# Weight sums of a ConvFFN by accumulating DMA in DRAM instead of on GpSimd, in a hybrid attention, retention and ConvFFN layer

## The chip, the core and the metric

The kernel runs on one core of one Trainium2 chip. The metric is device time in microseconds (us), the median of several runs. Engines are called as in the profile: PE (TensorE), PEld (its weight loads), DVE (VectorE), ACT (ScalarE), POOL (GpSimd) and SP (SyncE, which here only issues DMAs).

## The reference

One layer on 1024 latent tokens and 256 context tokens, D = 1024, all in float32: a modulated RMSNorm, one input projection that feeds a neighbourhood attention (8 heads of 64) and a retention in both directions (4 heads, 128 wide for q and k, 256 for v, chunks of 128), two projections merged by sigmoid gates, an output projection and a residual. Then the ConvFFN, which the change is about:

```python
def _conv_ffn(h, w_up, conv_w, conv_b, w_down):
    ...
    return (jax.nn.silu(a) * val) @ w_down
```

`a` and `val` are the two halves of `h @ w_up` (D_FF = 2816 columns each) after a depthwise convolution of width 3 along the tokens; a gated residual and a final RMSNorm follow.

## The kernel before, in words

**Precision.** Each float32 operand is split into a high and a low part (`split`: a cast on ACT, L86, and a subtraction on DVE, L87), and each product is three matmuls (high x high, high x low, low x high). A split needs the whole block in SBUF first: a load by SP, then L86, then L87, then PE.

**Strassen's scheme.** The gates, the up and the down projection multiply 2x2 blocks by seven products instead of eight. That needs sums of weight blocks and sums of activations. For the up projection `Seven.load` (L1379) loads four 128x512 blocks of w_up per unit through SP (`ur_load`) and POOL makes the four sums s1 to s4 (L1383 to L1386, tile `s`). The blocks and the sums of the up stage share a pool of 12 buffers (tag `r`). The first two of 22 units are computed plainly (`PLAIN`), 20 by Strassen; each has seven products (`step(0)` to `step(6)`) of 12 matmuls, PE line L1374, and the units are interleaved by `interleaved`: a unit's first product stands between the later products of the one before. `step(0)` copies product 0 out of PSUM on ACT (L1408, tile `pu`). `comb` makes the sums T1 to T4 of the activations ready for it, by loads from d_t into the same 12 buffers and splits (tile `T`). `conv` (L1754) makes the convolution, and for the down projection POOL makes four sums `sa` (L1777) for each second unit of the later half.

**Sums for the down projection.** They are made ahead and kept in DRAM (d_w): `down_sums` loads the four blocks of one of 11 units into tile `pj` through SP, POOL makes four differences (L1249), SP stores them. It is a generator, one sum a call. Five units are drawn in the retention, four in the gates, two in the ret projection.

**The retention** runs in slots (`slot`, L1262): 40 of them with a head's front part (`head.front`: projections to q, k, v, the rotary embedding `r`, states), beside which goes the mix part of the head before (`mix_a`, `mix_b`, `mix_c`: Q and O products, the normalisation `mvr`, `o`). Heads have 10 steps each (2 of context, 8 of latent tokens). At the end of a slot, one call of `next(ret_sums)` makes one down sum; it is left out in the context slots of heads 1 to 3 and in each head's last three. In a slot POOL has, in its order, the sum of `r` (L1115), the down sum, two sums `SS` (L1166) and `mvr` (L1193). DVE waits for `mvr` in L1194, and DVE's work for the next `r` (L1112 to L1114) stands behind that in its queue; ACT's `kz` (L1134) waits for `r`. Where heads change, the next head's weights (`in_w_ret`, 8 blocks a head, three buffers `raw`) are loaded through SP and split into `wc` and `wx` just in time.

Every DMA of the kernel before is issued by SP. Each engine executes its own instructions in order.

Of the kernel before, what the change touches and what calls it, by code (L numbers as in the profile page):

```python
# [16 lines left out]
P = 128  # L17
# [23 lines left out]
def tile_hybrid_layer(ctx, tc: tile.TileContext, io, dbg=None):  # L41
# [13 lines left out]
    d_ada = dram.tile([32, P], F32, name="d_ada")  # L55
    d_gate = dram.tile([2 * KB, 2, P, 512], F32, name="d_gate")
# [10 lines left out]
    cpool.tile([P, 24], F32, name="pad")  # L67
# [1168 lines left out]
    NH = NF // 2  # L1236

    def down_sums(pool_, j0, j1, bufs=8):
        def load(j, n):
            t = pool_.tile([P, 512], F32, tag="pj", bufs=bufs, name="pj")  # L1240
            sync.dma_start(t, io["w_down"][n % 2, NH * (n // 2) + j])
            return t

        ts, store = [load(j0, n) for n in range(4)], None
        yield
        for j in range(j0, j1):
            nxt = []
            for n, (c, x, y, o) in enumerate(((1, 1, 0, 0), (3, 3, 1, 1), (2, 3, 0, 3), (4, 2, 3, 2))):
                late(pool.tensor_tensor(ts[o], ts[x], ts[y], ALU.subtract))  # L1249
                if store:  # L1250
                    sync.dma_start(*store)
                store = (d_w[j, c - 1], ts[o])
                if j + 1 < j1:
                    nxt.append(load(j + 1, n))
                yield
            ts = nxt
        sync.dma_start(*store)

    RET_SUMS, GATE_SUMS = 5, 9
    ret_sums = down_sums(rt, 0, RET_SUMS)  # L1260

    def slot(main, mix, head=None, i=None):  # L1262
# [79 lines left out]
    def hx_sums(k):  # L1342
# [6 lines left out]
        for c, o, x, y in (("T1", b11, b12, b11), ("T3", b12, b22, b12), ("T2", b22, b22, b11), ("T4", b21, b21, b22)):  # L1349
            late(vec.tensor_tensor(o, x, y, ALU.subtract))  # L1350
# [25 lines left out]
    class Seven:  # L1376
        loaded = False

        def load(self):  # L1379
# [4 lines left out]
            pool.tensor_tensor(self.s2, self.s1, self.a11, ALU.subtract)  # L1384
            pool.tensor_tensor(self.s3, self.a11, self.a21, ALU.subtract)
            pool.tensor_tensor(self.s4, self.a12, self.s2, ALU.subtract)  # L1386
# [10 lines left out]
        def add(self, b, half, bank, x):  # L1397
            vec.tensor_tensor(self.dst(b, half), bank, x, ALU.add)
            self.done(b, half)

        def step(self, n):
# [7 lines left out]
            elif n == 1:  # L1409
                self.prod(self.Y, self.s2, "T2", True, False)  # L1410
                vec.tensor_tensor(self.u2, self.Y, self.p1, ALU.add)
            elif n == 2:
                self.prod(self.Z, self.s1, "T1", True, False)
            elif n == 3:
                self.fetch(1, 1)
                self.prod(self.Y, self.s3, "T3", False, False)
                vec.tensor_tensor(self.u3, self.Y, self.p1, ALU.add)  # L1417
                self.add(1, 1, self.Z, self.u3)
# [4 lines left out]
            elif n == 5:  # L1423
                self.fetch(1, 0)
                self.prod(self.Y, self.a22, "T4", False, True)
                self.add(1, 0, self.Y, self.p1)
            else:
                self.fetch(0, 1)
                self.prod(self.Z, self.s4, "B22", False, True)
                self.add(0, 1, self.Z, self.u2)  # L1430
# [104 lines left out]
    gate_sums = down_sums(gr, RET_SUMS, GATE_SUMS)  # L1535
    steps = interleaved(0, len(gu))
    n0, fetched = steps.index((len(gu) - 1, 0)), None
    for n, (i, k) in enumerate(steps):
        gu[i].step(k)
        if n % 3 == 1:  # L1540
            next(gate_sums, None)
# [12 lines left out]
    for _ in gate_sums:  # L1554
        pass
# [28 lines left out]
    pjp = sb("out_sums", "right")  # L1584
    out_sums = down_sums(pjp, GATE_SUMS, NH, 7)
# [25 lines left out]
    for db in range(2, KB):  # L1611
        wp[db] = pret_load(db)
        merge_load(db)
        if db == 2:
            brow(0, gate1)
        for half in range(2):
            pret(db, half)
            next(out_sums, None)
    pjp.release()
# [40 lines left out]
    def norm_out(tb, xr):  # L1660
# [25 lines left out]
        vec.tensor_tensor(b11, b12, b11, ALU.subtract)  # L1686
        vec.tensor_tensor(b12, b22, b12, ALU.subtract)
        vec.tensor_tensor(b22, b22, b11, ALU.subtract)
# [65 lines left out]
    def conv(j, gate, value):  # L1754
# [19 lines left out]
        for c, x, y, o in ((S1, a21, a22, ALU.add), (S2, S1, a11, ALU.subtract), (S3, a11, a21, ALU.subtract), (S4, a12, S2, ALU.subtract)):  # L1774
# [312 lines left out]
```

## Time and profile before

| what | value |
|---|---|
| time before, median of 3 runs | 1766.24 us (1765.4 to 1766.25) |
| span of the profiled execution | 1759.2 us, 7.0 us under the median |
| mean granted clock of PE | 0.996 |
| gates, ret projection | 768 to 921 us, 921 to 1008 us |
| plain up units, Strassen up units | 1101 to 1148 us, 1148 to 1540 us |
| down projection, end | 1540 to 1759 us |
| read from and written to DRAM | 187.34 MB, 69.48 MB |

The span is from the first to the last instruction of one profiled execution. Busy times are of single engines and overlap. A matmul of 128x512 has about 0.39 us in the rows, but a new one starts every 0.23 us, since they are pipelined. "DMA to landing" is the time from the issue of a transfer until its data are there. A name like `ur<-in_w_up` is output tile and input.

### The profile page before, as it was taken

Reading aid. Unit: us, or ns where it says so; the run is one execution under the profiler, and the core shown is the slowest. Engines: PE = TensorE matmul, PEld = TensorE weight load, DVE = VectorE, ACT = ScalarE, POOL = GpSimd, SP = SyncE. Lnnn points to the kernel's source line nnn. Section 1 sums busy time; section 2 is a strip of 40 time slices with the busy share of each in tenths; the row PEclk is TensorE's granted clock in tenths of the full one; section 3 lists DMA queues with packets and bytes.
Section 4 is the critical chain, followed back from the end, with each engine's and each line's share of the span. In section 5 each row is a group of like instructions: output and inputs, shape, how many; then the busy total and the mean of one; then the engine's idle time right before and its main releaser. Section 6 shows DMA issues by size and latency. Waiting matters only on the chain.

```text
span 1759.2 us, 24801 instructions
## 1 busy us (share of the span) xinstructions
PE 1726.0 (98%) x8405; PEld 1429.3 (81%) x8405; DVE 1284.2 (73%) x2454; ACT 849.2 (48%) x1826; POOL 539.3 (31%) x455
## 2 busy tenths in 40 slices
PE   8999999999999999999999999989999999999997
PEld 4688988888888888778888888778888888788886
DVE  4778887756776766777665557868899889875755
ACT  5666666653443434443444324534444444554444
POOL 1000000003334343555413300165555655211444
PEclk9999999999999999999999999999999999999999
DMA  9143334342231212677557733733322332586754
GB/s 348 61 130 125 95 117 147 117 133 87 73 108 43 72 42 68 203 238 239 200 199 268 246 143 132 254 108 102 108 90 92 118 120 90 170 296 192 239 162 162
DMA packets 139408, 261.10 MB, mean 148 GB/s; under 512 B 15856, under 2 KB 28304, under 8 KB 139280
## 3 DMA queue, kind: packets, MB, share of 16 engines
q1 hardware_dynamic: 139280, 259.51, 44.3%
q8 instruction: 66, 1.08, 0.3%
q14 instruction: 62, 0.51, 0.1%
HBM read 187.34 MB, written 69.48 MB: 146 GB/s over the span
## 4 chain that ended last, share of the span: by engine, by line
PE 43%; issue 6%; DVE 4%; POOL 3%; DMA 1%; ACT 1%; SPq 0%; POOLq 0%; ACTq 0%; DVEq 0%
PE u L1374 30%; PE y L1374 4%; PE pr L112 2%; PE pr L111 2%; PE pr L110 2%; PE om L122 1%; PE om L121 1%; PE om L123 1%; POOL x L1902 1%; DVE wc L87 0%; DVE b L1350 0%; DVE v L1679 0%; POOL pd L1939 0%; DVE hxT L87 0%; POOL x L1947 0%
## 5 line engine op out<-in xcount | busy, mean ns | idle before, releaser
L1374 PE MATMUL u<-T,wc 128*128 128x512 f32 x960 | 227.1, 392 | 5.1 <-ACT pu L1408 5.1
L1374 PEld LDWEIGHTS u<-T,wc 128*128 128x128 f32 x960 | 180.6, 189 | 45.7 <-ACT pu L1408 7.9
L1374 PE MATMUL y<-wc,ahl 128*128 128x512 f32 x924 | 210.6, 389 | 2.7 <-DVE wc L87 1.8
L1374 PEld LDWEIGHTS y<-wc,ahl 128*128 128x128 f32 x924 | 173.3, 188 | 39.7 <-DVE wc L87 2.5
L87 DVE TENSOR_TENSOR wc<-ur,wc 128x512 fp32r<-128x512 f32 x137 | 122.7, 897 | 65.8 <-ACT wc L86 65.8
L86 ACT CAST wc<-ur 128x512 fp32r<-128x512 f32 x137 | 85.0, 621 | 129.7 <-PE y L1374 72.3
L111 PE MATMUL mm<-low,wc 128*128 128x512 f32 (+1 forms) x328 | 124.0, 378 | 0.0
L1374 PE MATMUL u<-h2a,wc 128*128 128x512 f32 x480 | 112.3, 389 | 0.7 <-DVE pu L1417 0.7
L110 PE MATMUL mm<-hx,wc 128*128 128x512 f32 x264 | 107.4, 407 | 0.2 <-ACT wc L589 0.2
L1374 PEld LDWEIGHTS u<-h2a,wc 128*128 128x128 f32 x480 | 90.0, 188 | 19.8 <-DVE pu L1417 1.2
L112 PE MATMUL mm<-hx,wc 128*128 128x512 f32 x264 | 105.2, 399 | 0.0
L86 ACT CAST wc<-s 128x512 fp32r<-128x512 f32 x80 | 49.7, 623 | 93.2 <-PE u L1374 88.3
L123 PE MATMUL mm<-wc,low 128*128 128x512 f32 (+1 forms) x240 | 91.2, 380 | 0.0
L1374 PE MATMUL u<-hxT,wc 128*128 128x512 f32 x384 | 89.6, 389 | 0.0
L1508 POOL TENSOR_TENSOR col<-col,bcol 128x32 f32<-128x32 f32 x1 | 0.3, 253 | 280.7 <-DVE aw L538 280.7
L87 DVE TENSOR_TENSOR wc<-s,wc 128x512 fp32r<-128x512 f32 x80 | 83.5, 1046 | 3.8 <-ACT wc L86 3.4
L1374 PEld LDWEIGHTS u<-hxT,wc 128*128 128x128 f32 x384 | 72.1, 188 | 14.9
L87 DVE TENSOR_TENSOR wc<-raw,wc 128x512 fp32r<-128x512 f32 x92 | 68.0, 746 | 17.7 <-ACT wc L86 17.7
L121 PE MATMUL mm<-wc,hx 128*128 128x512 f32 x192 | 75.2, 392 | 0.6 <-ACT r L1105 0.6
L122 PE MATMUL mm<-wc,hx 128*128 128x512 f32 x192 | 75.2, 392 | 0.0
L1383 POOL TENSOR_TENSOR s<-ur 128x512 f32<-128x512 f32 x20 | 35.7, 1783 | 126.3 <-DVE wc L87 68.7
L86 ACT CAST wc<-raw 128x512 fp32r<-128x512 f32 x92 | 56.8, 621 | 33.0 <-PE pr L112 6.0
(393 smaller groups left out, 4671.3 us busy)
## 6 DMA issues: line engine op xcount, KB each, us to landing
ur<-in_w_up SPq DMA_DIRECT2D x80, 256.0 KB, 2.9
ur<-d_a SPq DMA_DIRECT2D x77, 256.0 KB, 3.1
aw<-in_w_ada SPq DMA_DIRECT2D x32, 512.0 KB, 3.3
pj<-in_w_down SPq DMA_DIRECT2D x44, 256.0 KB, 5.2
d_w<-pj SPq DMA_DIRECT2D x44, 256.0 KB, 2.0
d_a<-sa SPq DMA_DIRECT2D x44, 256.0 KB, 2.0
ur<-d_w SPq DMA_DIRECT2D x44, 256.0 KB, 3.8
d_a<-at SPq DMA_DIRECT2D x33, 256.0 KB, 2.7
```

The source lines that it names most:

```text
L86: act.copy(hi, src)
L87: (lo_eng or vec).tensor_tensor(lo, src, hi.bitcast(F32), ALU.subtract)
L110: pe.matmul(out, wh, xh, start=k == 0, stop=False)
L111: pe.matmul(out, wh, xl, start=False, stop=False)
L112: pe.matmul(out, wl, xh, start=False, stop=k == n - 1)
L121: pe.matmul(out, ah, bh, start=first, stop=False)
L122: pe.matmul(out, ah, bl, start=False, stop=False)
L123: pe.matmul(out, al, bh, start=False, stop=last)
L1374: pe.matmul(out, a, b, start=first and n == 0, stop=last and n == 2, skip_group_check=True)
L1383: pool.tensor_tensor(self.s1, self.a21, self.a22, ALU.add)
L1508: pool.tensor_tensor(col[:, 16:48], col[:, 16:48], bcol[:, 16:48], ALU.add)
L1902: pool.tensor_tensor(z, z, fg[:, gs(dh)], ALU.mult)
```

## The change

1. `down_sums` and its three uses are gone. `block_sums` takes their place: a job is four blocks and four places in DRAM; four plain DMAs copy blocks from DRAM to DRAM (`copy_of`, 16 rows of 16 KB, 256 KB each), and four accumulating DMAs add another block, or an earlier sum, onto them (`sum_of`, 32 rows of 8 KB). All eight are issued by POOL. The generator spreads each job over three rounds, so that an addition comes at least four issues after what it needs.
2. Twelve units of the up projection (`PRE`) and three of the down projection are such jobs in the retention, 15 x 8 = 120 issues, three in each of the 40 slots, context slots and last slots too. `puts` first copies 128x1 from the slot's `r0[i]` into a tile `tick` on POOL, which ties the issues to the slot, and then issues.
3. The other eight jobs of the down projection stand beside the up projection: after products 1 and 3 of each unit POOL copies 128x1 from `u2` or `u3` and issues two.
4. `Up.load` of those twelve units loads seven ready blocks (three of them raw, four from the new DRAM tensor `d_s`) through SP and gives POOL nothing to sum. The last eight units have POOL's four sums as before.
5. DMA can add but not subtract, so signs change: `block_sums` adds, and the sums of activations, the evacuations of products (`add`, u2, u3) and the end of the down projection add or subtract the other way. Their number and shapes stay.

```diff
+    d_s = dram.tile([12, 4, P, 512], F32, name="d_s")
...
-    cpool.tile([P, 24], F32, name="pad")
+    tick = cpool.tile([P, 24], F32, name="pad")[:, 0:1]
...
+    NH, PLAIN, PRE, RET_DOWN = NF // 2, 2, 12, 3
+    seq = [j + NH * i for j in range(NH) for i in range(2)]
+
+    def block_sums(jobs):
+
+        def add(out, src):
+            late(pool.dma_start(out, src, accum_op=ALU.add, max_dma_last_dim=8192))
+
+        def copy_of(n, c):
+            d, x, y, z, w = jobs[n]
+            late(pool.dma_start(d[c], (y, z, z, w)[c]))
+
+        def sum_of(n, c):
+            d, x, y, z, w = jobs[n]
+            add(d[c], (x, d[0], y, d[1])[c])
+
+        jobs = list(jobs)
+        for n in range(len(jobs) + 2):
+            for f, m, c in ((copy_of, n, 0), (sum_of, n - 1, 0), (copy_of, n, 2), (sum_of, n - 2, 3), (copy_of, n, 1), (sum_of, n - 1, 2), (copy_of, n, 3), (sum_of, n - 1, 1)):
+                if 0 <= m < len(jobs):
+                    yield f(m, c)
+
+    def up_jobs():
+        for n in range(PRE):
+            a = {(b, i): io["w_up"][seq[PLAIN + n], b, i] for b in range(2) for i in range(2)}
+            yield [d_s[n, c] for c in range(4)], a[1, 1], a[1, 0], a[0, 0], a[0, 1]
+
+    def down_jobs(j0, j1):
         for j in range(j0, j1):
...
+            b = {(r, c): io["w_down"][c, NH * r + j] for r in range(2) for c in range(2)}
+            yield [d_w[j, c] for c in range(4)], b[0, 0], b[0, 1], b[1, 1], b[1, 0]
+
+    def puts(it, src, n):
+        late(pool.tensor_copy(tick, src))
+        for _ in range(n):
+            next(it, None)
+
+    ret_sums = block_sums([*up_jobs(), *down_jobs(0, RET_DOWN)])
...
-            if i < NCB + NTB - 3 and (head.h == 0 or i >= NCB):
-                next(ret_sums, None)
+            puts(ret_sums, head.r0[i][:, 1, 0:1], 3)
...
+        def load(self):
+            n = self.n - PLAIN
+            if n >= PRE:
+                return super().load()
+            self.loaded = True
+            self.a11, self.s2, self.s1, self.s3, self.a12, self.a22, self.s4 = map(ur_load, (self.src[0, 0], d_s[n, 1], d_s[n, 0], d_s[n, 2], self.src[0, 1], self.src[1, 1], d_s[n, 3]))
...
+    up_sums = block_sums(down_jobs(RET_DOWN, NH))
     for i, n in interleaved(PLAIN, NF):
         units[i].step(n)
+        if n in (1, 3):
+            puts(up_sums, (units[i].u2 if n == 1 else units[i].u3)[:, 0:1], 2)
```

What stands in the engines' queues, at three places. First POOL in one retention slot with a mix part, before:

```order
L1115 TENSOR_TENSOR r_7262<-r_7262,r_7263 128x256
L1249 TENSOR_TENSOR pj<-pj 128x512
L1166 TENSOR_TENSOR SS<-st,SS 128x256
L1166 TENSOR_TENSOR SS<-run,SS 128x256
```

and such a slot after the change, from `r` to the next `r` (`pad` is the tile of `tick`; lines are those of the changed kernel, L1116 for L1115, L1167 for L1166, L1194 for L1193):

```order
L1116 TENSOR_TENSOR r_6264<-r_6264,r_6265 128x256
L1270 COPY pad<-r_6181 128x1
L1247 DMA d_s<-in_w_up 16x4096
L1243 DMA d_s<-in_w_up 32x2048
L1247 DMA d_s<-in_w_up 16x4096
L1167 TENSOR_TENSOR SS<-st,SS 128x256
L1167 TENSOR_TENSOR SS<-run,SS 128x256
L1194 TENSOR_TENSOR mvr<-mvr,mhalf 128x1
L1116 TENSOR_TENSOR r_6366<-r_6366,r_6367 128x256
```

The down sum between `r` and `SS` has given its place to the copy and three issues.

Second, SP at the start of the Strassen units, before, with what each row waits for (the last loads of the T sums, unit 2's four blocks, then unit 3's):

```order
L1735 DMA ur<-d_t 128x512 [waits DMAHW5_49,DVE_49]
L1735 DMA ur<-in_w_up 128x512 [waits DMAHW6_49,DVE_49]
L1735 DMA ur<-in_w_up 128x512 [waits DMAHW7_49,DVE_49]
L1735 DMA ur<-in_w_up 128x512 [waits DMAHW0_49,DVE_49]
L1735 DMA ur<-in_w_up 128x512 [waits DMAHW1_49,DVE_49]
L1766 DMA d_a<-at 128x512 [waits DMAHW2_49,DVE_49]
L1735 DMA ur<-in_w_up 128x512 [waits DMAHW6_49,DMAHW3_49,Pool_49]
```

and after (seven blocks of unit 2, then unit 3's first):

```order
L1739 DMA ur<-d_t 128x512 [waits DMAHW5_49,DVE_49]
L1739 DMA ur<-in_w_up 128x512 [waits DMAHW6_49,DVE_49]
L1739 DMA ur<-d_s 128x512 [waits DMAHW7_49,DMASW2_49,DVE_49]
L1739 DMA ur<-d_s 128x512 [waits DMAHW0_49,DMASW5_49,DVE_49]
L1739 DMA ur<-d_s 128x512 [waits DMAHW1_49,DMASW0_49,DVE_49]
L1739 DMA ur<-in_w_up 128x512 [waits DMAHW2_49,DVE_49]
L1770 DMA d_a<-at 128x512 [waits DMAHW3_49,DVE_49]
L1739 DMA ur<-in_w_up 128x512 [waits DMAHW4_49,Activation_49]
L1739 DMA ur<-d_s 128x512 [waits DMASW6_49,DMAHW5_49,DVE_49,Activation_49]
L1739 DMA ur<-in_w_up 128x512 [waits DMAHW6_49,DVE_49]
```

The wait for POOL (`Pool_49`) ahead of unit 3's first load is gone; waits for POOL's transfers of the retention (`DMASW`) stand at the loads from `d_s`.

Third, POOL beside the up projection after the change (before, four sums `s` a unit and the four `sa` stood here):

```order
L1270 COPY pad<-pu 128x1
L1243 DMA d_w<-d_w 32x2048
L1247 DMA d_w<-in_w_down 16x4096
L1270 COPY pad<-pu 128x1
L1243 DMA d_w<-in_w_down 32x2048
L1247 DMA d_w<-in_w_down 16x4096
...
L1781 TENSOR_TENSOR sa<-at 128x512
L1781 TENSOR_TENSOR sa<-sa,at 128x512
```

Each unit has two copies and four issues where its four sums were, until the last eight units, which keep them.

More of the change, by code (lines that the diff above doesn't have):

```diff
@@ L1233, in done @@
             return self.n >= NTB + 2
[L1236 to L1245, printed above, removed]
-        for j in range(j0, j1):
[L1247 to L1257, printed above, removed]
@@ L1938, in tile_hybrid_layer @@
         pool.tensor_tensor(u2[b], u2[b], gate2[:, gs(1)], ALU.mult)
-        pool.tensor_tensor(u2[b], u2[b], rows_of(b, 1), ALU.add)
+        pool.tensor_tensor(u2[b], rows_of(b, 1), u2[b], ALU.subtract)
     steps(4, range(NH), True, False)
```

47 lines of the change are left out of this document (17 added, 30 removed).

## Prediction, made blind

> **What bounds the kernel now.** I read the page's first part, then busy time by stage, then the waits of PE, and only then the other engines, in the stages that the change touches.
>
> ```profile
> span 1759.2 us, 24801 instructions
> PE 1726.0 (98%) x8405; PEld 1429.3 (81%) x8405; DVE 1284.2 (73%) x2454; ACT 849.2 (48%) x1826; POOL 539.3 (31%) x455
> ...
> 381.00:714.00 333.00, 331.69 (x1749) 283.53 (x1748) 226.38 (x716) 137.23 (x393) 115.04 (x150) 1.00 0.26 82
> ...
> 921.00:1008.00 87.00, 87.00 (x385) 72.07 (x384) 46.34 (x67) 35.21 (x60) 29.92 (x22) 1.00 0.76 256
> ...
> 1148.00:1540.00 392.00, 386.11 (x1689) 316.90 (x1688) 342.37 (x350) 178.87 (x250) 204.61 (x117) 1.00 0.35 113
> ```
>
> The last three rows are stages: the stretch, its length, the busy time of PE, PEld, DVE, ACT and POOL with counts, PE's granted clock, the DMA share and GB/s. PE is busy 98% of the span, so a sum that goes from POOL or SP is worth only the PE stall behind it. The retention (381 to 714 us) holds 1.3 us of PE idleness, the ret projection (921 to 1008), where down sums run now, none, the up projection (1148 to 1540) 5.9. Those 5.9 are one wait (row: who waited for whom, total, times, longest):
>
> ```profile
> PE u L1374 <- ACT pu L1408: 5.1, 1, 5.1
> ```
>
> The rows of that place are start, length, engine, line, operation, and in brackets the idle time ahead; first PE, then POOL, SP and ACT, and the clock in three stretches behind it.
>
> ```profile
> 1147.63 2.88 PE L1374 MATMUL u<-h2a,wc 128*128 128x512 f32 x12
> ...
> 1156.57 6.82 PE L1374 MATMUL u<-T,wc 128*128 128x512 f32 x22 [5.15 <-ACT pu L1408]
> ...
> 1139.52 5.42 POOL L1383 TENSOR_TENSOR s<-ur 128x512 f32<-128x512 f32 x1 [33.12 <-DMA ur<-in_w_up]
> 1145.02 1.72 POOL L1384 TENSOR_TENSOR s<-s,ur 128x512 f32<-128x512 f32 x1
> 1146.70 1.29 POOL L1385 TENSOR_TENSOR s<-ur 128x512 f32<-128x512 f32 x1
> ...
> 1148.02 8.22 SPq L1735 DMA_DIRECT2D ur<-in_w_up  x7
> ...
> 1146.78 1.87 ACT L86 CAST wc<-s 128x512 fp32r<-128x512 f32 x3 [4.78 <-POOL s L1384]
> 1152.85 0.62 ACT L86 CAST wc<-ur 128x512 fp32r<-128x512 f32 x1 [4.21 <-DMA ur<-in_w_up]
> ...
> 1155.93 0.58 ACT L1408 COPY pu<-u 128x512 f32<-128x512 f32 x1
> ...
> 1156.00:1158.00 2.00, 1.43 (x3) 1.16 (x4) 2.00 (x3) 1.03 (x3) 1.24 (x1) 0.62 0.47 122
> 1158.00:1160.00 2.00, 2.00 (x6) 1.59 (x5) 2.00 (x3) 0.00 (x0) 0.00 (x0) 0.53 0.51 137
> 1160.00:1165.00 5.00, 5.00 (x23) 4.13 (x22) 2.76 (x4) 1.25 (x2) 4.90 (x3) 1.00 0.39 145
> ```
>
> The first Strassen unit is late by its sums. POOL's first sum takes 5.42 us instead of 1.3 to 1.7. SP cannot send the next unit's loads until 1148.02, when POOL's third sum has let a buffer of the full pool go. ACT stands 4.78 us for the second sum, then 4.21 us for a load of the next unit, which stands in its queue ahead of the copy at 1155.93 that PE needs. PE idles 5.15 us and then runs at a granted clock of 0.62 and 0.53 until about 1160. Twelve matmuls at full clock take 2.88 us, a pitch of (2.88 - 0.39) / 11 = 0.226 us, so the 22 behind the stall should take 21 x 0.226 + 0.39 = 5.1 us and took 6.82. The wait thus costs 5.15 + 1.7 = **6.8 us**.
>
> The Trainium skill (TensorE: Matmul & The Clock Gate, Part 1: The HAM clock gate) says that a PE idle for a window of some 3.4 us falls to half clock. The 5.15 us gap followed by 0.53 agrees. By that rule a remainder of this stall under 3.4 us would cost its length alone.
>
> **The change, part by part.** *Up start.* Units 2 and 3 now load seven ready blocks each; no POOL sum and no release by POOL stands in SP's or ACT's way. Seven blocks of the first unit leave five of the twelve buffers to the second unit's loads, where four raw blocks, four sums and the wait for POOL stood. The order of PE's products is the same, and ACT's 4.78 and 4.21 us of idleness, 9.0 together, both go, which is more than the 5.15 that PE lost. What could be late next there are DVE's splits of the same tiles, which follow ACT's casts. I take the whole 6.8 us as the gain, with 0 as its other end.
>
> *Gates and ret projection.* PE has no idleness to give back there (87.00 of 87.00), so taking down sums, their loads and stores away is worth nothing.
>
> *Retention.* POOL gains three DMA issues and one 128x1 copy in each of 40 slots and loses a sum in 20. Here is one slot with a retention head beside another head's front; all its rows are POOL but the last two (DVE, PE). The fence behind it holds three groups: the sums of r over all four heads, the row nearest to the 128x1 copy (count, busy us, mean ns), and the only dynamic DMA queue.
>
> ```profile
> 496.64 0.73 POOL L1115 TENSOR_TENSOR r<-r,r 128x256 f32<-128x256 f32 x1 [2.11 <-DVE r L1114]
> 497.33 1.29 POOL L1249 TENSOR_TENSOR pj<-pj 128x512 f32<-128x512 f32 x1
> 500.36 0.73 POOL L1166 TENSOR_TENSOR SS<-init,SS 128x256 fp32r<-128x256 f32 x1 [1.75 <-ACT SS L1165]
> 501.05 0.74 POOL L1166 TENSOR_TENSOR SS<-run,SS 128x256 fp32r<-128x256 f32 x1
> 501.75 0.55 POOL L1193 TENSOR_TENSOR mvr<-mvr,mhalf 128x1 f32<-128x1 f32 x1
> 504.41 0.74 POOL L1115 TENSOR_TENSOR r<-r,r 128x256 f32<-128x256 f32 x1 [2.11 <-DVE r L1114]
> ...
> 502.33 0.41 DVE L1194 TENSOR_SCALAR o<-o,mvr 128x256 f32<-128x256 f32 x1 [0.98 <-POOL mvr L1193]
> ...
> 505.26 0.45 PE L121 MATMUL Q<-SS,qk 128*128 128x512 f32 x1
> ```
>
> ```profile
> L1115 POOL TENSOR_TENSOR r<-r,r 128x256 f32<-128x256 f32 x32 | 23.5, 735 | 115.1 <-DVE r L1114 115.1
> L1906 POOL TENSOR_SCALAR ssf<-ssf 128x1 f32<-128x1 f32 x8 | 3.0, 381 | 16.3 <-ACT xr L1897 16.3
> ...
> q1 hardware_dynamic: 139280, 259.51, 44.3%
> ```
>
> Between the end of r (497.37) and the start of SS (500.36) POOL has 2.99 us. The copy takes about 0.38 of it by the 128x1 row, which leaves 2.61 us for three issues, 0.87 us each. What one issue holds POOL for, call it X, no row shows: all 139280 packets went through the hardware queue. Past 0.87 us SS is late by 3X - 2.61; POOL's mvr comes straight behind SS, DVE's L1194 waits 0.98 us for mvr, and DVE's work for the next r is queued behind L1194, so the lateness adds up from slot to slot. PE first feels it when the sum of it passes the 505.26 - 501.79 = 3.47 us between SS and its use. Of 32 sums r, 24 are in slots of this kind (heads 1 to 3, eight in a row, with a long stretch between heads in which POOL catches up). The loss is 3 x (8 x (3X - 2.61) - 3.47): nothing up to X = 1.01, 13 us at 1.2.
>
> For X the lower end is SP's time for an issue, the upper the sum that POOL did in the slot, 1.29, or its mean over all 44, 1.43:
>
> ```profile
> 1140.20 0.33 SPq L1766 DMA_DIRECT2D d_a<-at  x1
> ...
> L1249 POOL TENSOR_TENSOR pj<-pj 128x512 f32<-128x512 f32 x44 | 62.7, 1426 | 7.5 <-DMA pj<-in_w_down 7.0
> ```
>
> An issue of 16 or 32 rows passes no 128x512 block through POOL; it is nearer to SP's 0.33 and to POOL's smallest instructions (0.38 and 0.55) than to 1.43. I take X at most 0.9 and the cost on this path as **0**, with 30 us (X = 1.43) as its far end.
>
> *Transfers in the retention.* 120 transfers of 256 KB, half of which also read their destination, add some (60 x 2 + 60 x 3) x 0.262 = 79 MB in 333 us, about 235 GB/s, to a stage that moved 82. The ret projection moved 256 without a PE stall, but at the change of heads PE waits directly for loads:
>
> ```profile
> PE mm L122 <- DVE wx L87: 0.7, 3, 0.2
> ...
> 518.04 1.25 ACT L86 CAST wc<-raw 128x512 fp32r<-128x512 f32 x2 [0.20 <-DMA raw<-in_w_ret]
> ...
> 523.62 0.63 ACT L86 CAST wx<-raw 128x512 fp32r<-128x512 f32 x1
> ...
> 524.68 0.68 DVE L87 TENSOR_TENSOR wx<-raw,wx 128x512 fp32r<-128x512 f32 x1
> ...
> 525.41 0.44 PE L122 MATMUL mm<-wx,hc 128*128 128x384 f32 x1 [0.22 <-DVE wx L87]
> ...
> DMA to landing us min/median/max: 2.5/2.6/3.7
> ```
>
> Two loads of in_w_ret follow each other through the same buffer, and PE waits 0.22 us at the end: there is next to no slack. Their landing times around this change are 2.5 to 3.7 us; the worst is 1.1 above the median. Before, the down sums were kept out of these slots; now they are not. Both loads at the worst give 2.2 us a change of heads, less the 0.43 us that lie between ACT's cast (until 524.25) and DVE's split (524.68), so 5.3 us over three changes; with none it is 0. POOL's transfers fill about half of a slot, so one load in two meets one: 1.1 - 0.43, three times, **2.0 us**.
>
> *Waits of the issues.* An accumulating transfer waits for the ones more than a slot (7.8 us) ahead of it. The nearest landings are
>
> ```profile
> pj<-in_w_down SPq DMA_DIRECT2D x44, 256.0 KB, 5.2
> d_w<-pj SPq DMA_DIRECT2D x44, 256.0 KB, 2.0
> ```
>
> 5.2 and 2.0 us, so POOL should not stand there. *Beside the up projection* POOL (204.6 of 392 us busy) loses 48 sums, at least 48 x 1.29 = 62 us, and gains 64 issues (58 at 0.9) and 40 copies (15): about even, with the sums of the last eight units needed long after their loads. I count nothing.
>
> **The sum.** 1759.2 - 6.8 + 2.0 = 1754.4 us of span. The median of the runs, 1766.2, is 7.0 us above the profiled span; I let that much lie around the new span too: **1761.4 us**.
>
> **Rivals.** *(a) POOL's issues stretch the retention slots*, the one that ends slower. It decides from X = 1.01; at 1.2 the kernel takes 1761.4 + 13 = 1774, at 1.43 1791. For it: POOL has already a sum of 5.42 us, against 1.3 to 1.7, when DVE was splitting T beside it, so POOL can be held up by DVE, and each slot has DVE at work. Against it: the sum in this slot took 1.29 us with DVE at work too. Spread evenly from 0.33 to 1.43, six tenths of X would lie under 1.01. *(b) The loads at the change of heads take the gain back*: 5.3 instead of 2.0 gives 1764.7. The 0.22 us waits speak for it; that the price takes the worst landing twice at each of three places speaks against. *(c) The stall at 1156 stays*, because another load or a DVE split comes as late: the change does not do there what it would; 1766.2 + 2.0 = 1768.2. Against it stand ACT's 9.0 us of idleness. *(d) DVE holds each issue for several times its length*: as the first sum was, 5.42 / 1.29 = 4.2 times, an issue of 0.55 us would take 2.3, and the loss be 3 x (8 x (6.9 - 2.61) - 3.47) = 93 us, 1854. The 1.29 us of the sum in this very slot speak against it. The Trainium skill (SBUF — State Buffer, SBUF: two separate sides) names such a hold: a GpSimd-issued DMA of about 620 ns takes about 3100 ns while a DVE copy keeps the shared port. No run shown so far has such an issue, so no number of mine rests on it.
>
> **How the numbers follow.** Forecast (1759.4 with no loss at the heads, to 1762.7) 0.48; (a) 0.22; (b) 0.20; (c) 0.06; (d) 0.04. A measurement of this kernel tells about 0.2%, 3.5 us, from no change, so the bounds are 1762.7 and 1769.8. Faster: the forecast, 0.48. Same: (b) and (c), 0.26. Slower: (a) and (d), 0.26. The range starts just under the case with no loss, 1759.4, and reaches into (a) to X = 1.33, 1784; what lies above is some 0.1, and some 0.1 below or in between is doubt in the terms themselves.
>
> **What would show it.** Right: no PE wait over 1 us at the start of the up projection and a clock of 1.00 there; POOL's gap from r to SS not longer than 2.99 us; the change of heads at most 1 us longer. Wrong: the slot's period over 7.8 us with PE waiting for SS or kz (a); PE waits of 1 to 2 us on wx or wc at each head (b); ACT again idle before the copy of pu (c).

## The result and the profile after

The changed kernel takes 1784.91 us (median; 1783.14 to 1794.34), the kernel before in the same comparison 1765.82. The medians differ by 19.1 us. The ratio of the runs is 1.0126, with an interval of 1.0100 to 1.0152, which is 18 to 27 us. The forecast of 1761.4 us was wrong in sign, and the time lies just above the range that ended at 1784.

These are the rows of the changed kernel that answer to those of before: the span and busy times, then the same three stages (retention, ret projection, Strassen units of the up projection; length, busy time of PE, PEld, DVE, ACT, POOL, PE's granted clock, DMA share, GB/s).

```profile
span 1784.1 us, 24998 instructions
PE 1734.6 (97%) x8405; PEld 1436.5 (81%) x8405; DVE 1245.1 (70%) x2454; ACT 850.3 (48%) x1826; POOL 537.7 (30%) x627
...
382.65:740.40 357.75, 340.22 (x1748) 290.41 (x1747) 215.46 (x716) 137.12 (x393) 175.90 (x290) 0.98 0.55 135
952.30:1039.30 87.00, 87.00 (x386) 72.03 (x385) 47.50 (x67) 35.68 (x60) 20.25 (x14) 1.00 0.65 210
1179.30:1564.70 385.40, 384.24 (x1687) 315.64 (x1687) 319.63 (x348) 176.89 (x247) 187.73 (x176) 1.00 0.58 177
```

The up projection went from 392.0 to 385.4 us, and PE idles 1.2 us there instead of 5.9. The retention went from 333.0 to 357.8: PE idles 17.5 us instead of 1.3, and its busy time grew by 8.5 because the clock fell to 0.98 on average. The ret projection is as long as before. Nearly the whole change of time lies in the retention, the up projection and one smaller place.

PE executes the same 8405 matmuls in all these kernels in nearly the same order, so the start of the n-th matmul in one trace less that in another shows where time went. Worked out so against the profiled execution of before, in us (bounds at 381, 714, 790, 921, 1140 and 1165 us of before; the experiments of the next section are already in it):

| kernel | to 381 | retention | to 790 | gates | to 1140 | start of up | rest |
|---|---|---|---|---|---|---|---|
| changed | +1.6 | **+24.9** | +1.0 | **+3.8** | -0.1 | **-6.9** | +0.2 |
| e1_tiny | -2.5 | +4.3 | -0.1 | +1.8 | -0.1 | -6.9 | +3.1 |
| e2_copies | -0.1 | +6.3 | -0.7 | +4.0 | 0.0 | -6.9 | +3.4 |
| e3_rows2k | +1.7 | +23.0 | +1.7 | +2.0 | +0.5 | -6.9 | +0.7 |
| e4_midhead | +2.0 | +15.6 | +1.5 | +1.7 | +0.3 | -6.9 | -0.5 |
| e5_mid3 | -1.2 | +1.2 | +0.7 | +4.1 | +0.1 | -6.9 | +3.8 |
| e6_nobunch | +0.3 | +25.0 | +2.6 | +4.2 | -0.1 | -6.9 | +0.9 |
| e7_lean2 | +0.9 | +1.7 | +0.6 | 0.0 | +0.3 | -6.9 | +1.5 |
| e8_lean4 | -0.9 | +19.2 | +0.6 | 0.0 | -0.2 | -6.9 | +1.2 |
| e9_pin | -0.7 | +23.5 | -0.9 | 0.0 | -0.1 | -6.9 | +0.8 |
| e10_nolast | +0.2 | +1.4 | +1.5 | +1.8 | -0.2 | -6.9 | +1.3 |
| e11_nolast_pin | +0.5 | +1.8 | +1.7 | 0.0 | +0.9 | -6.9 | +1.1 |

The first column is code that no kernel here changes; its -2.5 to +2.0 us shows what single executions differ by. The last column varies by 4 us among the kernels, and nothing is read from it.

**The start of the up projection** is as forecast. PE of the changed kernel there:

```profile
1178.90 2.88 PE L1387 MATMUL u<-h2a,wc 128*128 128x512 f32 x12
1181.62 8.39 PE L1387 MATMUL u<-T,wc 128*128 128x512 f32 x36
```

No bracket stands behind the second row: the 36 matmuls follow at once, (8.39 - 0.39) / 35 = 0.229 us apart. Before, the first 38 matmuls from the unit's start took from 1147.63 to 1163.39, 15.8 us; here 38 take 37 x 0.228 + 0.39 = 8.8.

**The retention.** First what PE waited for there (who, for whom, total, times, longest), then how POOL's slot looks now, as in the slot shown of before:

```profile
PE mm L122 <- ACT wc L87: 5.8, 3, 3.3
PE mm L122 <- ACT wx L87: 5.6, 2, 4.3
PE dS L122 <- ACT kz L1135: 4.5, 2, 2.4
PE Q L123 <- POOL SS L1167: 0.7, 1, 0.7
```

```profile
581.17 0.74 POOL L1116 TENSOR_TENSOR r<-r,r 128x256 f32<-128x256 f32 x1 [2.18 <-DVE r L1115]
581.85 0.19 POOL L1270 COPY pad<-r 128x1 f32<-128x1 f32 x1
581.97 0.58 POOL L1247 DMA_DIRECT2D d_s<-in_w_up  x1
582.55 0.83 POOL L1243 DMA_DIRECT2D d_s<-in_w_up  x1
583.08 0.81 POOL L1247 DMA_DIRECT2D d_s<-in_w_up  x1
584.64 0.74 POOL L1167 TENSOR_TENSOR SS<-init,SS 128x256 fp32r<-128x256 f32 x1 [0.75 <-ACT SS L1166]
```

The three issues start 0.58 and 0.53 us apart, and SS starts 3.47 us behind r (ready when ACT is), where it was 3.72. The issues fit. What doesn't is the change of heads; here the third one, first ACT, then PE, POOL's issues in it, and the landing of the loads around it:

```profile
607.73 1.27 ACT L87 CAST wc<-raw 128x512 fp32r<-128x512 f32 x2 [4.98 <-DMA raw<-in_w_ret]
...
617.45 0.62 ACT L87 CAST wx<-raw 128x512 fp32r<-128x512 f32 x1 [4.45 <-DMA raw<-in_w_ret]
...
608.40 0.69 PE L122 MATMUL mm<-wc,hc 128*128 128x384 f32 x1 [3.26 <-ACT wc L87]
618.12 0.62 PE L122 MATMUL mm<-wx,hc 128*128 128x384 f32 x1 [4.29 <-ACT wx L87]
...
605.10 0.81 POOL L1243 DMA_DIRECT2D d_s<-in_w_up  x1
...
608.68 1.07 POOL L1247 DMA_DIRECT2D d_s<-in_w_up  x1
...
DMA to landing us min/median/max: 2.6/7.2/8.3
```

Six transfers of POOL, of which the first and the last are shown, start within 4 us, the loads into `raw` land after 7.2 us in the middle and 8.3 at most (2.7 and 4.3 at this change before), ACT waits 4.98 and 4.45 us for them and PE 3.26 and 4.29. The waits for kz are the same thing once removed: at 449.68 ACT's cast, which stands ahead of kz in its queue, waits 2.18 us for such a load. Ahead of the other, at 691.47, a cast waits 3.69 us for a load of in_w_gate, the first weights of the gates.

```profile
449.68 0.62 ACT L87 CAST wc<-raw 128x512 fp32r<-128x512 f32 x1 [2.18 <-DMA raw<-in_w_ret]
```

By the starts of the matmuls the 24.9 us are 4.1, 4.7 and 10.1 at the three head changes and 6.0 at the end of the last head, where the gates' weights are loaded. They are of two kinds. PE's waits for wc, wx and kz, 15.9 us in the rows above, are the late loads. The other kind is PE's clock: five of these stalls, of 2.43, 2.09, 3.26, 4.29 and 2.02 us, are each followed by 3.4 us at half clock. PE loses half of such a spell, 1.7 us, if it is busy all through it, so five make some 8.5 us, the amount by which its busy time grew. Here are the spells behind the stalls of 2.43 and 2.02 us, and one behind a stall of 1.91 us in the gates (columns as in the stages above, the clock third from the end):

```profile
451.00:454.40 3.40, 3.40 (x13) 3.40 (x12) 1.53 (x4) 0.96 (x3) 1.38 (x3) 0.50 0.99 278
693.30:696.70 3.40, 3.40 (x11) 2.79 (x12) 2.06 (x5) 1.20 (x5) 1.16 (x2) 0.50 0.58 121
945.90:949.30 3.40, 3.40 (x9) 2.63 (x9) 1.40 (x3) 1.62 (x3) 0.00 (x0) 0.50 0.83 286
```

**The end of the gates** has a new stall, in a stage in which POOL issues no transfer: PE waits once for DVE's `pu`, and SP's queue ahead of that shows why. The last row is the same place in the queue of before.

```profile
PE u L1387 <- DVE pu L1430: 1.9, 1, 1.9
...
929.41 0.86 SPq L1540 DMA_DIRECT2D orw<-d_orr  x2
930.32 0.45 SPq L1487 DMA_DIRECT2D o<-d_pn  x1
936.47 0.32 SPq L1495 DMA_DIRECT2D d_gate<-c  x1
936.88 0.87 SPq L1540 DMA_DIRECT2D orw<-d_orr  x2
...
901.38 1.97 SPq L1527 DMA_DIRECT2D orw<-d_orr  x4
```

Two of four loads `orw` stand behind a store that waits until 936.47 for ACT; in the queue of before all four stood in a row. `pu` stands in DVE's queue behind the splits of these loads. The stall of 1.91 us and the 1.7 us of slow clock behind it make the 3.8 of the table. In the kernels with 1.7 to 2.0 in that column the stall was 1.42 to 1.74 us and no slow clock followed; in those with 4.0 to 4.2 it was 2.10 to 2.35 us and the clock fell.

### The profile page after: what moved, and what is told of

Its sections match the earlier page's. It is cut to its first block, busy times and chain, and to the rows that moved or that the text cites. A ratio compares the mean times of both kernels' runs of the same rounds, so it can differ in the third digit from the quotient of the medians.

```text
span 1784.1 us, 24998 instructions
## 1 busy us (share of the span) xinstructions
PE 1734.6 (97%) x8405; PEld 1436.5 (81%) x8405; DVE 1245.1 (70%) x2454; ACT 850.3 (48%) x1826; POOL 537.7 (30%) x627
## 3 DMA queue, kind: packets, MB, share of 16 engines
q0 software_dynamic: 7360, 48.25, 12.1%
## 4 chain that ended last, share of the span: by engine, by line
PE 38%; issue 6%; DVE 5%; POOL 3%; DMA 2%; ACT 2%; SPq 0%; POOLq 0%; ACTq 0%; DVEq 0%
PE u L1387 24%; PE y L1387 4%; PE pr L112 2%; PE pr L111 2%; PE pr L113 2%; PE om L123 1%; PE om L124 1%; PE om L122 1%; DVE wc L88 1%; POOL x L1913 1%; DMA raw<-d_orr 1%; PE u L112 1%; PE u L113 0%; PE u L111 0%; DVE ta L1765 0%
## 5 line engine op out<-in xcount | busy, mean ns | idle before, releaser
L88 DVE TENSOR_TENSOR wc<-ur,wc 128x512 fp32r<-128x512 f32 x185 | 149.5, 811 | 75.7 <-ACT wc L87 75.5
L87 ACT CAST wc<-ur 128x512 fp32r<-128x512 f32 x185 | 114.8, 622 | 178.3 <-PE u L1387 100.5
L1781 POOL TENSOR_TENSOR sa<-at 128x512 f32<-128x512 f32 x22 | 37.3, 1695 | 138.3 <-DVE at L1767 138.3
L112 PEld LDWEIGHTS mm<-low,wc 128*128 128x128 f32 x328 | 63.1, 192 | 6.9
L88 DVE TENSOR_TENSOR ahl<-ur,ahl 128x512 fp32r<-128x512 f32 x77 | 64.1, 840 | 0.8 <-ACT ahl L87 0.7
```

The costliest lines, as they stand in the source:

```text
L87: act.copy(hi, src)
L88: (lo_eng or vec).tensor_tensor(lo, src, hi.bitcast(F32), ALU.subtract)
L112: pe.matmul(out, wh, xl, start=False, stop=False)
L1781: pool.tensor_tensor(prev[c], x, y, o)
```

## The experiments

Theory T: the transfers make the loads of in_w_ret land late where heads change, and PE waits for those. Rivals: P, POOL's issues themselves hold up r and SS there; Q, the long rows of the transfers block the short rows of the loads. Each edit is against the changed kernel unless said otherwise. Single runs were compared with a run of the kernel before on the same chip.

### e1_tiny: the issues without their bytes

```diff
+            small = slice(0, 16) if tiny[0] else slice(0, P)
-            late(pool.dma_start(out, src, accum_op=ALU.add, max_dma_last_dim=8192))
+            late(pool.dma_start(out[small], src[small], accum_op=ALU.add, max_dma_last_dim=8192))
```

(the copies likewise with `tiny[1]`, both only in the retention; the kernel leaves out these sums, and its units read raw blocks in their place)

> The changed kernel with every one of the 120 transfers of the retention cut to its first 16 rows of 512 (32 KB instead of 256), so POOL issues as many DMAs at the same places but they move an eighth; the twelve units and the three down jobs then read raw weight blocks in place of the sums (the sums are left out). Theory T (the transfers make the loads of in_w_ret land late at the change of heads): landing times back to about 2.6 to 3 us, the three head changes back from 23 to 29 us to about 19.5, the kernel near 1763 (before less 6.8 for the start of the up projection, plus 3.6 for the new stall at the end of the gates). Rival P (POOL's issues, six in a row at a head change, hold up r and SS): head changes stay at 23 to 29 us and the kernel near 1784.

Measured: 1760.91 us (before: median 1763.25 of 7). The retention's loss falls from 24.9 to 4.3 us; loads of in_w_ret land after 2.9 us (group median, 4.6 in the changed kernel). POOL issues as often and at the same places. So P is out for some 20 of the 25 us. The rest is not pursued; here the largest wait of PE in the head changes is 1.1 us for DVE's split of wx.

```profile
raw<-in_w_ret SPq DMA_DIRECT2D x32, 256.0 KB, 2.9
...
PE mm L123 <- DVE wx L88: 2.3, 3, 1.1
```

### e2_copies: only the plain copies keep their bytes

The same edit with `tiny` for the accumulating transfers alone, so that seven eighths of each accumulation are left out.

> The changed kernel with only the 60 accumulating transfers of the retention cut to 16 rows of 512; the 60 plain copies stay at 256 KB (three of four sums are left out). Theory T with each transfer weighing by its bytes moved (copy 2, accumulation 3): about 40% of the loss in the retention stays, some 8 to 10 us of 24, kernel near 1772. If the accumulations alone make the loads late, the head changes go back to 19.5 us (kernel near 1763); if the copies do it, they stay (1782).

Measured: 1767.26 us; the retention loses 6.3 us, 2.0 more than with both kinds cut. The copies are the small part, smaller than the 8 to 10 us that weighing by bytes gave. The software queue of DMA shows the kinds apart (packets, MB, share of 16 engines' span), first the changed kernel, then this one, then e1_tiny:

```profile
q0 software_dynamic: 7360, 48.25, 12.1%
```

```profile
q0 software_dynamic: 6400, 34.48, 7.9%
```

```profile
q0 software_dynamic: 6400, 20.72, 5.4%
```

12.1% of 1784.1 us is 215.9 us of all engines, 7.9% of 1765.5 is 139.5, 5.4% of 1759.1 is 95.0. Cutting 60 accumulations to an eighth saves 76.4 us, so one holds all 16 engines for about 76.4 / (60 x 7/8) = 1.46 us, if an eighth of a transfer takes an eighth of the time; a copy 44.5 / 52.5 = 0.85. Since the loss grows from 6.3 to 24.9 when the accumulations come back, it isn't in proportion to the engines' time (44.5 us for 2.0 us of loss, 76.4 for 18.6); the queue that the loads meet may have to be long before PE feels it, which is argued, not shown. Accumulations without copies were not tried.

### e3_rows2k: short rows

```diff
-            late(pool.dma_start(out, src, accum_op=ALU.add, max_dma_last_dim=8192))
+            late(pool.dma_start(out, src, accum_op=ALU.add, max_dma_last_dim=2048))
```

(the copies likewise)

> The changed kernel with the same bytes, but each transfer of POOL in 128 rows of 2 KB instead of 16 of 16 KB or 32 of 8 KB. Theory Q (the large rows stand ahead of the 2 KB rows of the loads on each DMA engine): landing times of in_w_ret fall to 3 to 4 us and half or more of the 24 us of the retention returns, kernel 1765 to 1772. Theory T (bytes and time on the DMA engines count, not the row): no gain, 1783 or more, and more if 128 descriptors hold POOL longer than the 0.53 us of now (above 1.01 us the slots stretch as well).

Measured: 1783.98 us, the retention 23.0 us longer, in_w_ret landing after 4.4 us (4.6). The length of the rows doesn't matter here; Q is out. 128 rows didn't stretch the slots between the head changes either.

### e4_midhead: five issues a slot, away from the head changes

```diff
-            puts(ret_sums, head.r0[i][:, 1, 0:1], 3)
+            if i < NCB + NTB - 3 and (head.h == 0 or i >= NCB):
+                puts(ret_sums, head.r0[i][:, 1, 0:1], 5 if head.h else 6)
```

> The changed kernel with no POOL transfer in the slots around a change of heads (the slots that the down sums used before), five instead of three in each of the 15 others of heads 1 to 3 and six in the seven of head 0; one down job fewer there (14 jobs). Theory T: loads of in_w_ret land in about 2.6 us again at the change, head changes near 19.5 us, kernel near 1764; what five issues cost in the middle is 5 x 0.53 + 0.19 = 2.85 us against 2.99 of room, nothing. Rival: the middle slots now stretch or their loads come late, and the loss only moves: 1775 or more.

Measured: 1774.9 us (1772.89 to 1780.73), ratio 1.0075 [1.0048, 1.0102]. The second and third head change take 19.7 and 19.5 us again (from one r to the next), but the loss moved, as the rival said. POOL of this kernel in two slots of head 0 shows a wait that my prediction had put at nothing. Behind it stand PE's largest waits in the retention and, from the changed kernel, the group with most of its waits of this kind:

```profile
428.63 0.35 POOL L1270 COPY pad<-r 128x1 f32<-128x1 f32 x1
433.02 0.79 POOL L1243 DMA_DIRECT2D d_s<-d_s  x1 [4.05 <-DMA d_s<-d_s]
...
442.77 0.79 POOL L1243 DMA_DIRECT2D d_s<-d_s  x1 [3.70 <-DMA d_s<-d_s]
...
PE tp L1124 <- POOL r L1116: 5.5, 6, 1.8
PE tpo L1201 <- DVE A L1175: 2.8, 4, 1.1
...
L1243 POOL DMA_DIRECT2D d_w<-d_w x22 | 18.0, 819 | 12.1 <-DMA d_w<-d_w 12.1
```

With six issues a slot, as head 0 has them, an accumulation comes less than a slot after the one that it needs, POOL stands 4.05 and 3.70 us for that to land, and r behind it is late. In the changed kernel the spacing keeps this small, not at nothing: POOL stands five times for one of its own transfers, 12.7 us in all, four of these where a list of jobs ends and the spacing with it. Nearly all of that is hidden; PE waits 0.7 us behind it, once, for SS.

### e5_mid3: three issues a slot, away from the head changes

```diff
-    NH, PLAIN, PRE, RET_DOWN = NF // 2, 2, 12, 3
+    NH, PLAIN, PRE, RET_DOWN = NF // 2, 2, 6, 2
...
-            puts(ret_sums, head.r0[i][:, 1, 0:1], 3)
+            if i < NCB + NTB - 3 and (head.h == 0 or i >= NCB):
+                puts(ret_sums, head.r0[i][:, 1, 0:1], 3)
```

> The changed kernel with three POOL transfers a slot as it has, but none in the slots around a change of heads, and so only eight jobs in the retention (six units of the up projection instead of twelve, two down jobs instead of three; the rest of the sums as the change makes them, on POOL or beside the up projection). Theory T (late loads at the change of heads are the whole loss of the retention, and only transfers near them make them late): retention as long as before within 3 us, the start of the up projection 6.8 us shorter, the end of the gates 3.6 us longer, kernel 1 to 4 us under before on the same chip. Rival (any three transfers a slot cost, wherever they stand): retention 10 us or more longer, kernel slower than before.

Measured: 1763.68 us of 10 runs against 1764.06 of 15; ratio 0.9998 [0.9989, 1.0008]. The retention is as long as before (+1.2 us) with 64 transfers in it, so transfers away from the loads cost nothing there, within the 2 us by which executions differ. The 6.9 us at the start of the up projection are there; 4.1 at the end of the gates take most of them back, and the profiled execution has 3.8 more in the last column. The kernel is not faster than before; 1 to 4 us less were expected.

### e6_nobunch: none in the context slots

```diff
-            puts(ret_sums, head.r0[i][:, 1, 0:1], 3)
+            if head.h == 0 or i >= NCB:
+                puts(ret_sums, head.r0[i][:, 1, 0:1], 3)
```

(with PRE = 10, RET_DOWN = 2)

> The changed kernel with no POOL transfer in the two context slots of heads 1 to 3, which stand right behind a last slot of the head before; the last three slots of each head keep theirs (96 issues, ten units and two down jobs). Theory T by queueing (six transfers within 3 us at each change, 3 x 1.46 + 3 x 0.85 = 6.9 us of all DMA engines' time, stand ahead of the loads): the loads land at 5 us at most and half or more of the 26 us of the retention goes, kernel 1766 to 1773. Rival (any transfer near the loads does it, not the number in a row): more than two thirds stays, 1777 or more.

Measured: 1787.78 us, the retention 25.0 us longer. My own version of T fails: six in a row are not needed. The three head changes lose 20 of these 25 us, against 18.9 in the changed kernel. The other 5 come at the end of the last head, where POOL stands 4.60 us for its own accumulation to land and r is late, the cost that e4_midhead shows.

### e7_lean2: the kernel before with only two units summed by DMA

Against the kernel before: its `down_sums` stay on POOL where they were, and 16 issues for units 2 and 3 stand in head 0 (with the signs of the changed kernel).

```diff
+            if head.h == 0 and i < NCB + NTB - 3:
+                puts(ups, head.r0[i][:, 1, 0:1], 3)
             if i < NCB + NTB - 3 and (head.h == 0 or i >= NCB):
                 next(ret_sums, None)
```

> The kernel before, with its down sums on POOL where they were, and only the first two Strassen units of the up projection summed by POOL's DMAs, 16 issues in the first seven slots of head 0. If the start of the up projection needs only these two units and the gain does not hang on the rest of the change: 6 to 7 us less than before on the same chip, no new stall at the end of the gates (SP's queue there is as before) and the changes of heads at 19.5 us. If the third unit's sums on POOL come late instead, the stall moves there and the gain is under 3 us.

Measured: 1758.01 us (1755.55 to 1759.22) against 1764.06; ratio 0.9965 [0.9951, 0.9978], 6.2 us less. The gain of the change needs 16 of its 184 issues. The slots of head 0 have a down sum too, but no mix part beside it.

### e8_lean4: four units, in slots that also have a down sum

```diff
-            if head.h == 0 and i < NCB + NTB - 3:
-                puts(ups, head.r0[i][:, 1, 0:1], 3)
+            if i >= NCB and i < NCB + NTB - 3:
+                puts(ups, head.r0[i][:, 1, 0:1], 2)
```

(against e7_lean2, with PRE = 4; the slots of heads 1 to 3 have a mix part as well)

> As the run with two units, but four units summed by POOL's DMAs, 32 issues, two a slot in the five middle slots of each head. Theory T: these are away from the loads, so the same time as with two units, within 2 us. Rival: two issues and a POOL sum in one slot (2 x 0.53 + 0.19 + 1.29 = 2.5 us of 2.99) stretch the slots; 5 us or more slower than with two units.

Measured: 1774.33 us; the retention 19.2 us longer. The slots stretch, as the rival said, but not by the time of the issues. Here are POOL's slot, DVE's two operations for kz in it, PE's largest wait, and ACT's cast that SS waits for:

```profile
491.95 0.74 POOL L1116 TENSOR_TENSOR r<-r,r 128x256 f32<-128x256 f32 x1 [2.18 <-DVE r L1115]
...
493.36 0.72 POOL L1268 DMA_DIRECT2D d_s<-in_w_up  x1
493.88 1.51 POOL L1251 TENSOR_TENSOR pj<-pj 128x512 f32<-128x512 f32 x1
497.14 0.74 POOL L1167 TENSOR_TENSOR SS<-st,SS 128x256 fp32r<-128x256 f32 x1 [1.76 <-issue]
...
493.16 2.65 DVE L1136 SCALAR_TENSOR_TENSOR kz<-r,dec,kz 128x128 fp32r<-128x128 f32 x2 [0.96 <-ACT kz L1135]
...
496.62 0.40 ACT L1166 CAST SS<-st 128x256 fp32r<-128x256 f32 x1
...
PE tpo L1201 <- DVE A L1175: 10.6, 10, 2.1
```

POOL is free again at 495.39, in time for SS at 3.7 us behind r (495.65). But DVE's kz, which starts at 493.16 beside POOL's issues and its sum, takes until 495.81, just past the end of the sum. DVE's A stands behind it, PE waits for A, ACT's casts come late, and SS with them. The group of kz in the retention (72 times; busy, mean ns) tells it for three kernels, before, changed and this one:

```profile
L1135 DVE SCALAR_TENSOR_TENSOR kz<-r,dec,kz 128x128 fp32r<-128x128 f32 x72 | 36.4, 532 | 20.9 <-ACT kz L1134 20.7
```

```profile
L1136 DVE SCALAR_TENSOR_TENSOR kz<-r,dec,kz 128x128 fp32r<-128x128 f32 x72 | 26.3, 373 | 25.5 <-ACT kz L1135 25.1
```

```profile
L1136 DVE SCALAR_TENSOR_TENSOR kz<-r,dec,kz 128x128 fp32r<-128x128 f32 x72 | 60.0, 857 | 22.1 <-ACT kz L1135 21.9
```

With issues alone kz takes 373 ns in the mean, with sums 532, with both 857. These means mix cases. Single operations that overlap no work of POOL, or its issues alone, take about 0.35 us in all three kernels; one that overlaps a down sum takes 0.92 to 0.98 us in the kernel before; one that overlaps a down sum and an issue takes 1.8 to 3.8 us here, 15 times. So it is POOL's sum that holds DVE, not POOL's issue; why the two together hold it longest is open. The Trainium skill (SBUF — State Buffer, Who interferes with whom) says that DVE and GpSimd share one pair of ports, which only one of them holds at a time. The trace agrees as far as the sums go.

### e9_pin: the order at the end of the gates

```diff
-            fetched = orr_load(g_raw("orw"), 0, n - n0 - 1 + KH)
+            fetched = orr_load(g_raw("orw"), 0, n - n0 - 1 + KH, lambda ins: ins)
```

> The changed kernel with one edit: the four loads orw at the end of the gates keep the place in SP's queue where the program names them, instead of two of them behind a store that waits for ACT. If the 2 us stall at 945 us and the slow clock after it (3.6 us in all) come from that order, which moved when the gates' down sums left, they go: from the ret stage on about 3.6 us less than the changed kernel, the retention as late as in it. If they come from something else that the change moved, the step of 3.6 us at the end of the gates stays.

Measured: 1777.05 us (before: one run, 1766.08). The step at the end of the gates is 0.0 instead of 3.8, the retention still 23.5 longer. The order of SP's queue was the cause there.

### e10_nolast and e11_nolast_pin: none in the last three slots

```diff
-            puts(ret_sums, head.r0[i][:, 1, 0:1], 3)
+            if i < NCB + NTB - 3:
+                puts(ret_sums, head.r0[i][:, 1, 0:1], 3)
```

(with PRE = 8, RET_DOWN = 2; the second with the edit of e9_pin as well)

> The changed kernel with no POOL transfer in each head's last three slots, but with them in the context slots behind the change (84 of 120 places, 80 issues, eight units and two down jobs). The run that left out the context slots alone still lost 26 us, so the last three slots, where six of the eight loads of in_w_ret are sent, should hold most of the loss: landing times near 3 us for those loads and under a third (8 us) of the retention's loss left, kernel 1763 to 1770. If it needs both left out, as in the run where the retention was as short as before, the loss stays above 15 us and the kernel above 1775.

> Both repairs together: no POOL transfer in each head's last three slots (80 issues, eight units and two down jobs in the retention), and the four loads at the end of the gates in the order of the program. If the loads at the change of heads and that order are all that the change cost, what is left is the gain at the start of the up projection, 6.8 us, less about 1 us for a late r at the end of the last head: 5 to 7 us less than before on the same chip, as the kernel with two units. If transfers in the other slots or beside the up projection also cost something, the gain is under 3 us.

Measured: e10_nolast 1760.68 us (before: one run, 1766.08), less than the 1763 to 1770 expected, the retention 1.4 us longer than before; e11_nolast_pin 1759.96 us (1756.58 to 1762.69) against 1765.19, ratio 0.9967 [0.9955, 0.9980]. Landing of in_w_ret and PE's largest wait in the retention of e10_nolast:

```profile
raw<-in_w_ret SPq DMA_DIRECT2D x32, 256.0 KB, 2.8
...
PE tp L1124 <- POOL r L1116: 1.2, 1, 1.2
```

The 23.5 us of the retention come from 36 of 120 issues: those in the three slots of each head in which most of the next head's weights (in the last head the gates' first) are loaded. Transfers in the slots just behind do no harm. That total numbers don't explain it, e6_nobunch shows: its 96 issues, with those slots among them, lose all of it, and the 80 here next to nothing. Both repairs together leave 5.2 us between the medians, within the 5 to 7 expected, with eight units and two down jobs summed in the retention and the rest beside the up projection. e7_lean2 and e11_nolast_pin are both faster than both kernels and can't be told apart.

## Why the prediction was wrong, point by point

- **The start of the up projection**: -6.8 us forecast, -6.9 in all twelve kernels of the table. Right, with its second part: the 1.7 us of slow clock behind the 5.15 us stall went with it. PE waits 1.2 us in the whole up projection.
- **POOL's issues**: at most 0.9 us forecast, mostly 0.48 to 0.61 measured from the start of one issue to that of the next (0.53 in the middle), so X was below 1.01. Single slots shifted by up to 0.3 us, but in heads 1 and 2 the eight r take 55.0 us from first to last, as before. Right. What the term left out is that POOL's work can also hold DVE: the sums that left the slots did so (kz 532 ns in the mean, 373 without them), and e8_lean4, which has both, lost 19.2 us while POOL itself had room.
- **Gates and ret projection**: nothing forecast, +3.8 measured, all of it at the end of the gates. The step "taking down sums, their loads and stores away is worth nothing" looked only at time to be gained. Taking instructions away moved the order in which the others stand, and SP's queue was not compared there (e9_pin).
- **Transfers in the retention**: this is the step that failed, "Both loads at the worst give 2.2 us a change of heads". 2.0 us forecast, 5.3 as the worst, 24.9 measured, of which 23.5 go with the issues of the last slots (e10_nolast). The mechanism of rival (b) was right, the size wrong: twelve times the forecast and nearly five times its worst. It was wrong in four ways. The worst landing was read from a place without such transfers (3.7 us); under them, at the third change, it is 7.2 in the middle and 8.3 at most. Eight loads go through three buffers, so more than two delays follow one another: ACT waits for in_w_ret seven times, 19.9 us in sum. The end of the last head, where the gates' weights are loaded just as late, was not counted as a place: 6.0 us. And the stalls bring the slow clock, 8.5 us in five spells. That last point was used for the gain and not for the loss.

```profile
ACT wc L87 <- DMA raw<-in_w_ret: 13.7, 5, 5.0
ACT wx L87 <- DMA raw<-in_w_ret: 6.2, 2, 4.5
...
604.00:614.00 10.00, 6.57 (x31) 5.75 (x29) 4.30 (x10) 3.64 (x9) 5.58 (x10) 0.83 0.94 228
```

  The last row, a stretch of the third head change, shows the DMA engines 94% busy. Three transfers a slot, half of them accumulations, hold all engines for about 1.5 x 1.46 + 1.5 x 0.85 = 3.5 us of 7.8. The estimate of "one load in two" fits that share; that it failed because a load waits for all that is queued, not for one transfer, is argued, not shown.
- **The slow clock**: The Trainium skill (TensorE: Matmul & The Clock Gate, Part 1: The HAM clock gate) gives idle windows of some 3.4 us as the trigger. The traces differ: the clock fell to half already behind stalls of 1.91, 2.02 and 2.09 us of the changed kernel. In the 13 traces, between 381 us and 1740 us, every stall over 2.2 us went with a spell of 3.4 or 6.8 us at half clock, and 10 of the 16 from 1.7 to 2.2 us did. So the prediction's sentence that a stall under 3.4 us would cost its length alone does not hold: the 1.91 us at the end of the gates cost 3.8.
- **Waits of the issues, and the issues beside the up projection**: nothing forecast. For PE nearly right with the spacing of the changed kernel, 0.7 us for SS. For POOL "should not stand there" was wrong: it stood 12.7 us in five waits. e4_midhead shows the cost with a closer spacing.
- **The 7.0 us around the span** were a mistake, without weight for the difference of 4.8 us that was forecast: the changed kernel's profiled execution has 1785.87 us and a span of 1784.1, so 1.8 lie around it. The profiled execution of before was then one of about 1761 us, at the lower end of its 1758.9 to 1767.7. The difference of the two profiles, 24.9 us, is for that reason above that of the medians, 19.1.
- **The rivals**: (a) didn't happen in this kernel, (b) did and was priced at 1764.7, (c) and (d) didn't. Eight of the 184 issue rows are longer than 1.1 us (2.09 at most), but they overlap, and the issues among them still start about half a us apart.

## What to carry to other kernels

A transfer that nobody waits for is paid by the load that someone does wait for: before moving traffic into a stage, find the loads there that are sent just in time, and keep the new transfers out of the slots in which these are sent; elsewhere in the same stage they were free. Price such a collision from a place of the trace with comparable DMA load, count all loads of the chain, and add the slow clock, 1.7 us here, if the stall that results is of about 2 us or more. Look also at which part of a change makes the gain: here 16 of 184 issues.

## What the runs showed of the hardware

- An accumulating DRAM to DRAM transfer of 256 KB held all 16 DMA engines for about 1.46 us, a plain one for about 0.85 (worked out under e2_copies); the length of the rows, 2 KB or 8 and 16 KB, made next to no difference to the loads beside it (landing after 4.4 and 4.6 us). That a DMA can't subtract was not tried.
- Issues of DMA by POOL in a row mostly started 0.48 to 0.61 us apart with 16 or 32 rows, and 0.51 to 0.60 with 128 (e3_rows2k). With 128 rows POOL also stood idle in front of five issues, 3.11 us at most, for something that no row shows.
- A POOL sum of two 128x512 blocks in SBUF slowed DVE's two-input operation beside it (kz about 0.35 us without one, 0.92 to 0.98 beside one, 1.8 to 3.8 beside one with an issue); issues alone did not.
- PE's granted clock fell to 0.50 for 3.4 or 6.8 us with every PE stall over 2.2 us, and with 10 of 16 from 1.7 to 2.2 us (all 13 traces, 381 to 1740 us).
